# An MLP up projection in seven products: the next pair's first product put ahead of the last two, and its side work spread out

## The chip, the cores and the metric

One core of a Trainium2 chip runs the whole kernel. The metric is the device time of one execution in microseconds (us); lower is better. The kernel is compared before and after one edit, each as the median of several runs.

## The reference

One layer of a decoder with two branches (a gated linear recurrence and sparse attention), their merge, an output projection, and then an MLP, over 1024 prompt rows and 32 sample rows in float32. The edit touches the MLP alone:

```
x = x + m @ w_o
h2 = _rmsnorm(x, norm2)
x = x + jnp.square(jax.nn.relu(h2 @ w_up)) @ w_down
```

h2 is 1056 x 1024, w_up 1024 x 4096, w_down 4096 x 1024. A last RMSNorm follows.

## The kernel before

Everything is held transposed: features on the 128 partitions, the T = 1056 tokens along the free dimension. float32 products are made of three float32r products: each operand is split into a high part (a cast, on ScalarE) and a low part (the value less the high part, on VectorE), and high x high, high x low and low x high are added in PSUM.

The up projection uses a scheme with 7 products for 2 x 2 blocks in place of 8. The four blocks are the two halves of the contraction (512 features each) by the two halves of the tokens (TH = 528). The operands on the token side (OPS) are made once by `combine`: for each of 4 steps of the contraction 7 combinations of the blocks, split into high and low, 28 tiles in all; those of step 0 and the P1 of step 1 lie in h2a, those of step 3 in h2b, the rest in tiles of their own, which the trace calls h2P. So a run of P1 reads h2a in 6 of its 12 matmuls, that of any other product in 3.

The loop runs over 16 pairs of 128 output features. For pair i two raw blocks of w_up are loaded (`up_raw`, on SP's queue), four sums or differences of their quarters are taken on VectorE (`up_sums`, tiles ws), and seven weight tiles are split (`up_split`). Weight tile g may be split once product g - 6 is done, since there are six buffers. A pair's seven products stand in ORDER: P1, P2, P6, P5, P7, P4, P3. Each is made for two chunks of TC = 264 tokens, 4 steps x 3 matmuls a chunk: a run of 12 matmuls, 168 matmuls a pair.

PSUM has three kinds of tiles here. pua holds two banks, one for each chunk; P1 goes there, and P6, P7 and P4 add to it, one behind the other. pub (one tile a chunk) takes P2; puc (one a chunk) takes P5 and then P3 on top. There are two tiles of each kind, so two pua, with two banks each. After P1, P6 and P7 ScalarE copies the running sum out (tile uu, line 1307), and VectorE builds the output from it: hd0 low = P2 + the copy of P1 (line 1309), hd1 high = P5 + the copy of P7 (1311), hd1 low from the sum in pua after P4, through relu and times rb2 (1313), hd0 high = P3 + the copy of P6 (1315). rb2 is the RMSNorm factor of the token, from `rb_chunk` (tile rb2p, which in the stage's start takes one of the pua places). Then hd is multiplied by rb2 with relu where that is still due (1339), squared (1340) and stored (1341), and the down projection reads it back.

The programmer's listing is not the order of an engine's queue. The framework's planner takes, by its own cost model, the first instruction in the listing that is ready; instructions in `high_priority` go ahead. It also puts in the waits, and it counts a tile of PSUM as one: the first matmul into either bank of pua waits for the last copy in the listing ahead of it, out of either bank. SBUF tiles called U are places of one size, given back to the end of a list and taken from its front.

Of the kernel before, what the change touches and what calls it, by code (L numbers as in the profile page):

```python
# [10 lines left out]
F32 = mybir.dt.float32  # L11
F32R = mybir.dt.float32r
# [30 lines left out]
ORDER = ("P1", "P2", "P6", "P5", "P7", "P4", "P3")  # L43

# [44 lines left out]
def hybrid_step(ctx: ExitStack, tc, x_prompt, x_sample, cache_k, cache_v, cache_idx_k, state_hgrn,  # L89
# [20 lines left out]
    def ps_s(name):  # L110
        return psum.tile([128, 2, 512], F32, name=name, tag="s", bufs=2)
# [1048 lines left out]
    def up_raw(i):  # L1160

        rs_ = []
        for h in range(2):
            if h == 1 and i % 2 == 0:
                r = wp.tile([128, 4, 256], F32, name="wu1", tag="wr", bufs=1)
            else:
                r = U.get([128, 4, 256], F32, "wu0")
            nc.sync.dma_start(r, w_up[0][h * 512:(h + 1) * 512, i * 256:(i + 1) * 256]
                              .rearrange("(k p) m -> p k m", p=128))
            rs_.append(r)  # L1170
        return rs_
# [3 lines left out]
    for j in (0, 4, 1, 5, 2, 6, 3, 7):  # L1175
# [3 lines left out]
        if j == 7:  # L1179
            raw[0] = up_raw(0)  # L1180
# [36 lines left out]
    def up_sums(i):  # L1217

        r = raw[i]
        s12, s34 = (U.get([128, 2, 4, 128], F32, "ws") for _ in range(2))  # L1220
        a11, a21 = r[0][:, :, :128], r[0][:, :, 128:]
        a12, a22 = r[1][:, :, :128], r[1][:, :, 128:]
# [5 lines left out]
        return ({"P1": a11, "P2": a12, "P6": s12[:, 1], "P5": s12[:, 0], "P7": s34[:, 0], "P4": a22, "P3": s34[:, 1]},  # L1228
                [s12, s34, r[0]] + ([r[1]] if i % 2 else []))

    SRC = {}
    wus = Ring(U, 2)
    us = Ring(U, 2)
    W = {}

    def up_split(g):

        i, q = g // 7, ORDER[g % 7]
        if g % 6 < 4:
            w = wp.tile([128, 2, 4, 128], F32R, name="wu" + q, tag=("wl", "wh")[g % 6 // 2], bufs=2)  # L1240
        else:
            w = wus.get([128, 2, 4, 128], F32R, "wu" + q)
        with tc.high_priority():
            nc.scalar.copy(w[:, 0], SRC[i][0][q])
            nc.vector.tensor_tensor(w[:, 1], SRC[i][0][q], w[:, 0].bitcast(F32), op=ALU.subtract)
        W[g] = w
        if g % 7 == 6:
            U.put(*SRC[i][1])
# [12 lines left out]
    SRC[0] = up_sums(0)  # L1261
    for g in range(6):
        up_split(g)
    raw[1] = up_raw(1)
# [7 lines left out]
    for i in range(16):  # L1272
        pa = ps_s("pua")
        pb, pc = [ps_g("pub") for _ in range(2)], [ps_t("puc") for _ in range(2)]
        banks = [{"P1": pa[:, c, :TC], "P2": pb[c][:, :TC], "P5": pc[c][:, :TC]} for c in range(2)]
        for c in range(2):
            banks[c]["P6"] = banks[c]["P7"] = banks[c]["P4"] = banks[c]["P1"]
            banks[c]["P3"] = banks[c]["P5"]
        uu = [us.get([128, 4, TC], F32, "uu") for _ in range(2)]
        hd = [U.get([128, T], F32, f"hd{e}") for e in range(2)]  # L1280

        def product(q, c, ks):
            ps = banks[c][q]
            sl = slice(c * TC, (c + 1) * TC)
            for k in ks:
                x, w = OPS[k, q], W[i * 7 + ORDER.index(q)]
                for n_, (a, b) in enumerate(((0, 0), (0, 1), (1, 0))):
                    nc.tensor.matmul(ps, w[:, a, k], x[:, b, sl], start=(q in "P1P2P5" and k == n_ == 0),  # L1288
                                     stop=(k == 3 and n_ == 2), skip_group_check=True)

        if i == 0:

            for q in ("P1", "P2", "P5"):
                for c in range(2):
                    product(q, c, range(3))
            prb = ps_s("rb2p")
            for c in range(2):
                rb_chunk(prb[:, c, :CH], slice(c * CH, (c + 1) * CH))
        for n, q in enumerate(ORDER):
            for c in range(2):  # L1300
                ps = banks[c][q]
                sl = slice(c * TC, (c + 1) * TC)
                s2 = slice(TH + c * TC, TH + (c + 1) * TC)
                product(q, c, (3,) if i == 0 and q in ("P1", "P2", "P5") else range(4))
                with tc.high_priority():
                    if q in ("P1", "P6", "P7"):
                        nc.scalar.copy(uu[c][:, "P1P6P7".index(q) // 2], ps)  # L1307
                    if q == "P2":
                        nc.vector.tensor_tensor(hd[0][:, sl], ps, uu[c][:, 0], op=ALU.add)
                    elif q == "P7":  # L1310
                        nc.vector.tensor_tensor(hd[1][:, s2], banks[c]["P5"], uu[c][:, 2], op=ALU.add)
                    elif q == "P4":
                        nc.vector.scalar_tensor_tensor(hd[1][:, sl], ps, 0.0, rb2[:, sl], op0=ALU.max, op1=ALU.mult)
                    elif q == "P3":
                        nc.vector.tensor_tensor(hd[0][:, s2], ps, uu[c][:, 1], op=ALU.add)
            if i == 0 and n == 2:
                rb_chunk(prb[:, 0, :CH], slice(2 * CH, T))
            if i * 7 + n + 6 < 112:
                up_split(i * 7 + n + 6)
            if n == 0 and i < 15:  # L1320
                if i < 14:
                    raw[i + 2] = up_raw(i + 2)
                SRC[i + 1] = up_sums(i + 1)
            if i == 15:
                for k in range(4):
                    if 8 <= k * 7 + n < 21:
                        U.put(OPS[k, q])
                if n == 0:
                    lo0 = hid_load(0, lambda e, a: U.get([128, T], F32R, "hdl"))
                elif n == 1:  # L1330
                    hi0 = [U.get([128, T], F32R, "hdh") for _ in range(4)]
                    for l_, h_ in zip(lo0, hi0):
                        hid_split(l_, h_)
                elif n < 6:
                    x1_again(2)
                if n == 5:
                    wd0 = wload(w_down[0, :512, :], 0, 4, 256, "wd")
# [115 lines left out]
```

## Time and profile before

| | |
|---|---|
| median of 3 runs | 1837.68 us (1835.46 to 1846.53) |
| the profiled execution | 1841.7 us, span of the trace 1840.0 us |
| mean granted TensorE clock | 0.982 |
| TensorE busy | 1755.7 us (95%) |
| VectorE, ScalarE busy | 1145.2 us (62%), 767.3 us (42%) |
| up projection, first to last matmul | about 1091.9 to 1447.1 us |

A busy engine in the profile has an instruction in it; TensorE's instructions overlap, so that a matmul is shown for 0.28 us where one starts each 0.12 us. Idle time stands with the instruction that came behind it, and with it what released that instruction. A line such as L1288 is a line of the kernel.

### The profile page before, as it was taken

The numbers are of one execution on the slowest core, as the hardware profiler recorded it, in microseconds if no ns is written. First come the engines' busy times: TensorE is split into PE (matmuls) and PEld (weight loads), VectorE is DVE, ScalarE is ACT, GpSimd is POOL, SyncE is SP. The second block draws the span as 40 slices with busy tenths as digits, with TensorE's granted clock in tenths as the row PEclk, the third lists the DMA queues.
The fourth block names the chain that finished last, engine by engine and source line by source line (L and its number), as shares of the span: only waits on it lengthen the run. The fifth ranks groups of instructions, "written<-read, shape, count | busy, mean of one in ns | idle before, by whom it ended". The sixth has DMA issues, their size and how long they took to land.

```text
span 1840.0 us, 29018 instructions
## 1 busy us (share of the span) xinstructions
PE 1755.7 (95%) x11644; PEld 1693.3 (92%) x11644; DVE 1145.2 (62%) x2534; ACT 767.3 (42%) x1330; POOL 188.1 (10%) x212
## 2 busy tenths in 40 slices
PE   6999999998999989979999999999999999999997
PEld 5999999998999988867899999999999899999997
DVE  7276485645799897955646668555555634444435
ACT  5456465244578822343523554333333501111112
POOL 1100000022000015631100330000000000000000
PEclk8999999899999999989999999999999999999999
DMA  4411121231223224542543332332223712222212
GB/s 152 139 50 47 48 63 53 54 86 34 80 76 100 71 82 134 178 161 71 157 137 104 105 128 71 108 114 94 94 94 100 300 58 94 94 94 94 93 46 95
DMA packets 135846, 181.78 MB, mean 99 GB/s; under 512 B 9056, under 2 KB 111232, under 8 KB 135712
## 3 DMA queue, kind: packets, MB, share of 16 engines
q1 hardware_dynamic: 115232, 125.88, 21.3%
q0 software_dynamic: 13424, 44.87, 7.9%
q10 hardware_dynamic: 7056, 9.18, 1.4%
q8 instruction: 91, 1.49, 0.3%
q14 instruction: 43, 0.35, 0.1%
HBM read 128.96 MB, written 48.11 MB: 96 GB/s over the span
## 4 chain that ended last, share of the span: by engine, by line
PE 46%; DMA 6%; DVE 4%; issue 4%; ACT 2%; POOL 2%; SPq 0%; DVEq 0%; ACTq 0%; POOLq 0%
PE pua L1288 10%; PE pd L144 6%; PE pd L146 6%; PE pd L145 6%; PE puc L1288 5%; PE pub L1288 2%; PE po L146 2%; PE po L145 2%; PE po L144 2%; DMA qb<-q_d 2%; DMA hdn<-hid_d 1%; POOL qb L889 1%; PE po L856 1%; DMA vpg<-in_cache_v_dram,ids 1%; PE wap L144 1%
## 5 line engine op out<-in xcount | busy, mean ns | idle before, releaser
L144 PE MATMUL pd<-hdn,wdh 128*128 128x352 f32 (+3 forms) x672 | 218.9, 326 | 3.0 <-DVE x L1381 2.8
L145 PE MATMUL pd<-hdn,wdh 128*128 128x352 f32 (+3 forms) x672 | 215.7, 321 | 0.0
L146 PE MATMUL pd<-hdn,wdl 128*128 128x352 f32 (+3 forms) x672 | 215.6, 321 | 0.0
L1381 DVE TENSOR_TENSOR x<-x,pd 128x352 f32<-128x352 f32 (+3 forms) x192 | 99.7, 519 | 174.6 <-PE pd L146 174.5
L144 PEld LDWEIGHTS pd<-hdn,wdh 128*128 128x128 f32 x672 | 126.2, 188 | 6.0 <-DVE x L1381 4.7
L145 PEld LDWEIGHTS pd<-hdn,wdh 128*128 128x128 f32 x672 | 126.3, 188 | 1.2
L146 PEld LDWEIGHTS pd<-hdn,wdl 128*128 128x128 f32 x672 | 126.0, 188 | 1.3
L144 PE MATMUL wgt<-hh,wgth 128*128 128x352 f32 x384 | 126.6, 330 | 0.0
L146 PE MATMUL wgt<-hh,wgtl 128*128 128x352 f32 x384 | 124.8, 325 | 0.0
L145 PE MATMUL wgt<-hl,wgth 128*128 128x352 f32 x384 | 124.6, 325 | 0.0
L136 ACT CAST wdh<-wdr 128x1024 fp32r<-128x1024 f32 x28 | 29.5, 1053 | 215.9 <-PE pd L145 206.3
L1288 PE MATMUL pua<-h2P,wuP 128*128 128x264 f32 x672 | 102.9, 285 | 0.0
L1288 PE MATMUL pua<-h2a,wuP 128*128 128x264 f32 x480 | 83.2, 292 | 14.0 <-ACT uu L1307 12.7
L747 ACT ACTIVATE jkA<-sc,bstg 128x1024 bf16<-128x1024 bf16 (+5 forms) x93 | 87.3, 939 | 19.6 <-DVE bstg L766 6.8
L1288 PEld LDWEIGHTS pua<-h2P,wuP 128*128 128x128 f32 x672 | 90.6, 189 | 0.0
L1288 PEld LDWEIGHTS pua<-h2a,wuP 128*128 128x128 f32 x480 | 67.2, 189 | 20.5 <-ACT uu L1307 19.1
L742 DVE TENSOR_SCALAR_CACHE_REDUCE jkD<-sc,bstg 128x768 bf16<-128x768 f32 (+3 forms) x96 | 84.4, 879 | 1.1
L1307 ACT COPY uu<-pua 128x264 f32<-128x264 f32 x96 | 36.3, 378 | 109.5 <-PE pua L1288 85.1
L144 PEld LDWEIGHTS wgt<-hh,wgth 128*128 128x128 f32 x384 | 72.1, 188 | 2.5 <-issue 1.7
L145 PEld LDWEIGHTS wgt<-hl,wgth 128*128 128x128 f32 x384 | 72.3, 188 | 1.4 <-issue 0.5
L146 PEld LDWEIGHTS wgt<-hh,wgtl 128*128 128x128 f32 x384 | 72.2, 188 | 1.4 <-issue 0.8
L1288 PE MATMUL pua<-h2b,wuP 128*128 128x264 f32 x384 | 68.7, 286 | 1.8 <-DVE h2b L1139 1.8
(782 smaller groups left out, 4954.1 us busy)
## 6 DMA issues: line engine op xcount, KB each, us to landing
hid_d<-hd SPq DMA_DIRECT2D x32, 528.0 KB, 2.7
wu<-in_w_up_dram SPq DMA_DIRECT2D x32, 512.0 KB, 3.9
wdr<-in_w_down_dram SPq DMA_DIRECT2D x32, 512.0 KB, 3.4
hdn<-hid_d SPq DMA_DIRECT2D x28, 528.0 KB, 4.6
sg_d<-gst ACTq DMA_DIRECT2D x48, 176.0 KB, 2.4
wgtr<-in_w_in_dram SPq DMA_DIRECT2D x16, 512.0 KB, 3.9
qb<-q_d POOLq DMA_DIRECT2D x16, 512.0 KB
wasg<-sg_d SPq DMA_DIRECT2D x8, 528.0 KB, 5.0
```

The costliest lines, as they stand in the source:

```text
L136: nc.scalar.copy(wh, raw)
L144: nc.tensor.matmul(ps, wh, xh, start=(k == 0), stop=False)
L145: nc.tensor.matmul(ps, wh, xl, start=False, stop=False)
L146: nc.tensor.matmul(ps, wl, xh, start=False, stop=(k == n - 1))
L742: nc.vector.tensor_scalar(jkD[:, 0, :L], SC[i], s if isinstance(s, float) else s[:, a:a + 1], 0.0, op0=op, op1=ALU.add, accum_out=out[:, a ...
L747: nc.scalar.activation(jkA[:, 0, :(i + 1) * 128], src(i), AF.Sign, bias=thr[:, a:a + 1], accum_out=cnt[:, a:a + 1])
L856: nc.tensor.matmul(po[:, :128], vt[:, j, :], pT[:, j, :], start=(j == 0), stop=(j == i))
L889: nc.gpsimd.tensor_tensor(qb, kp[:, 1:2, :].to_broadcast([128, 2, 512]), qb, op=ALU.mult)
L1288: nc.tensor.matmul(ps, w[:, a, k], x[:, b, sl], start=(q in "P1P2P5" and k == n_ == 0), stop=(k == 3 and n_ == 2), skip_group_check=True)
L1307: nc.scalar.copy(uu[c][:, "P1P6P7".index(q) // 2], ps)
L1381: nc.vector.tensor_tensor(x1[:, sl], x1[:, sl], ps, op=ALU.add)
```

## The change

The seven products of all pairs become one list, SEVEN: P1 of pair 0, then for each pair P2, P6, P5, P7, P1 of the next pair, P4, P3. Weight tiles follow this list. uu becomes two tiles that stay for the whole stage, one a chunk, with four places: P6 and P7 have one each, and P1 has two, used in turn. The tiles of the sums (s12, s34) stay as well, and the four sums of the next pair are taken one at a time behind P2, P6, P5 and P7. The two raw loads of a pair are asked for separately: the first behind the next P1, the second behind P3. The products with rb2 and the squares are made for each half of hd as soon as it is there, behind P2, P7, P4 and P3, and a store follows P4 (hd1) and P3 (hd0).

```diff
+SEVEN = [(0, "P1")] + [(i + (q == "P1"), q) for i in range(16) for q in ("P2", "P6", "P5", "P7", "P1", "P4", "P3")
+                       if not (i == 15 and q == "P1")]
...
-    us = Ring(U, 2)
+    uu = [U.get([128, 4, TC], F32, "uu") for _ in range(2)]
+    s12, s34 = (U.get([128, 2, 4, 128], F32, "ws") for _ in range(2))
...
+    def up_sum(i, n):
+
+        p = parts(i)
+        o, x, y, op = (("P5", "a21", "P4", ALU.add), ("P6", "P5", "P1", ALU.subtract),
+                       ("P7", "P1", "a21", ALU.subtract), ("P3", "P2", "P6", ALU.subtract))[n]
         with tc.high_priority():
-            nc.vector.tensor_tensor(s12[:, 0], a21, a22, op=ALU.add)
-            nc.vector.tensor_tensor(s12[:, 1], s12[:, 0], a11, op=ALU.subtract)
-            nc.vector.tensor_tensor(s34[:, 0], a11, a21, op=ALU.subtract)
-            nc.vector.tensor_tensor(s34[:, 1], a12, s12[:, 1], op=ALU.subtract)
+            nc.vector.tensor_tensor(p[o], p[x], p[y], op=op)
...
-        i, q = g // 7, ORDER[g % 7]
+        i, q = SEVEN[g]
...
-    raw[1] = up_raw(1)
+    up_raw(1, 0)
+    up_raw(1, 1)
...
+    def bank(i, q, c):
+
+        if q in ("P1", "P6", "P7", "P4"):
+            if (i, 0) not in BANK:
+                t = ps_s("pua")
+                BANK[i, 0] = [t[:, e, :TC] for e in range(2)]
+            return BANK[i, 0][c]
...
+    def relu2(i, e, sl, scaled):
+        t = hd[i][e][:, sl]
+        if not scaled:
+            nc.vector.scalar_tensor_tensor(t, t, 0.0, rb2[:, sl], op0=ALU.max, op1=ALU.mult)
+        nc.scalar.activation(t, t, AF.Square)
...
+    for g, (i, q) in enumerate(SEVEN):
+        if q == "P2":
+            hd[i] = [U.get([128, T], F32, f"hd{e}") for e in range(2)]
+        for c in range(2):
...
+            product(g, c, (3,) if g in (0, 1, 3) else range(4))
+            ps, u1 = bank(i, q, c), 3 * (i % 2)
+            with tc.high_priority():
+                if q in ("P1", "P6", "P7"):
+                    nc.scalar.copy(uu[c][:, {"P1": u1, "P6": 1, "P7": 2}[q]], ps)
...
+        if g + 6 < len(SEVEN):
+            up_split(g + 6)
+        if 1 <= g % 7 <= 4 and g // 7 < 15:
+            up_sum(g // 7 + 1, g % 7 - 1)
+
+        p = g // 7 + (g % 7 == 5)
+        for h in {0: (0, 1) if g == 0 else (1,), 5: (0,)}.get(g % 7, ()):
+            if p < 16 and (h == 0 or p % 2):
+                U.put(raw[p][h])
+            if p + 2 < 16:
+                up_raw(p + 2, h)
+        if q in ("P2", "P7", "P4", "P3"):
+            e, sl = {"P2": (0, LO), "P7": (1, HI), "P4": (1, LO), "P3": (0, HI)}[q]
+            relu2(i, e, sl, q == "P4")
+            if q in ("P4", "P3"):
+                nc.sync.dma_start(hid_d[2 * i + e], hd[i][e])
+                U.put(hd[i][e])
...
-        for e, sl in ((1, slice(TH, T)), (0, slice(0, T))):
-            nc.vector.scalar_tensor_tensor(hd[e][:, sl], hd[e][:, sl], 0.0, rb2[:, sl], op0=ALU.max, op1=ALU.mult)
-            nc.scalar.activation(hd[e], hd[e], AF.Square)
-            nc.sync.dma_start(hid_d[2 * i + e], hd[e])
-            U.put(hd[e])
```

What the last pair did besides, loading the first part of the down projection, stands behind the same products of the list, counted from its end.

## Rows read from the trace of the kernel before

**Rows 1.** The page, its first part: busy time and share of each engine.

```profile
PE 1755.7 (95%) x11644; PEld 1693.3 (92%) x11644; DVE 1145.2 (62%) x2534; ACT 767.3 (42%) x1330; POOL 188.1 (10%) x212
```

**Rows 2.** Windows: start, 13 pairs, end. Columns: stretch, length, busy time by engine.

```profile
1091.90:1134.96 43.06, 39.73 (x297) 37.81 (x295) 40.78 (x76) 22.45 (x48) 3.10 (x1) 0.96 0.29 100
...
1134.96:1416.85 281.89, 272.04 (x2187) 267.58 (x2186) 160.60 (x274) 107.11 (x195) 0.00 (x0) 1.00 0.30 99
...
1416.85:1447.15 30.30, 27.70 (x218) 26.64 (x217) 16.36 (x26) 12.35 (x19) 4.01 (x8) 1.00 0.63 234
```

**Rows 3.** Groups by line, 1134.96 to 1416.85: busy us, mean ns, idle before.

```profile
L1288 PE MATMUL pua<-h2a,wuP 128*128 128x264 f32 x390 | 67.0, 290 | 9.9 <-ACT uu L1307 9.9
...
L1244 ACT CAST wuP<-ws 128x512 fp32r<-128x512 f32 x52 | 32.3, 622 | 38.9 <-PE pub L1288 17.8 <-DVE ws L1225 13.7 <-PE puc L1288 6.9
...
L1340 ACT ACTIVATE hd<-hd 128x1056 f32<-128x1056 f32 x26 | 28.3, 1087 | 19.5 <-DVE hd L1339 19.5
...
L1224 DVE TENSOR_TENSOR ws<-wu,wu 128x512 f32<-128x512 f32 x13 | 8.9, 688 | 0.2
```

**Rows 4.** Waits, same stretch: waiter, releaser, us in total, times, longest.

```profile
ACT uu L1307 <- DVE hd L1315: 22.7, 13, 2.0
...
PE pua L1288 <- ACT uu L1307: 9.9, 21, 0.5
```

**Rows 5.** Timeline of TensorE, about one pair: start, us, engine, line, idle before.

```profile
1214.82 0.88 PE L1288 MATMUL pua<-h2a,wuP 128*128 128x264 f32 x6
...
1216.26 0.53 PE L1288 MATMUL pua<-h2a,wuP 128*128 128x264 f32 x3
...
1218.35 0.63 PE L1288 MATMUL pua<-h2a,wuP 128*128 128x264 f32 x3 [0.47 <-ACT uu L1307]
...
1220.55 0.63 PE L1288 MATMUL pua<-h2a,wuP 128*128 128x264 f32 x3 [0.47 <-ACT uu L1307]
...
1222.12 0.78 PE L1288 MATMUL pub<-h2a,wuP 128*128 128x264 f32 x5
...
1225.05 0.52 PE L1288 MATMUL pua<-h2a,wuP 128*128 128x264 f32 x3
...
1226.51 0.53 PE L1288 MATMUL puc<-h2a,wuP 128*128 128x264 f32 x3
...
1227.97 0.52 PE L1288 MATMUL pua<-h2a,wuP 128*128 128x264 f32 x3
```

**Rows 6.** Timeline of ScalarE, same stretch.

```profile
1217.92 0.38 ACT L1307 COPY uu<-pua 128x264 f32<-128x264 f32 x1 [0.55 <-PE pua L1288]
1220.12 0.38 ACT L1307 COPY uu<-pua 128x264 f32<-128x264 f32 x1 [1.82 <-PE pua L1288]
...
1229.33 0.38 ACT L1307 COPY uu<-pua 128x264 f32<-128x264 f32 x1 [1.72 <-DVE hd L1315]
```

**Rows 7.** Timeline of TensorE, the stage's end (the first form three times).

```profile
1433.86 0.63 PE L1288 MATMUL pua<-h2a,wuP 128*128 128x264 f32 x3 [0.47 <-ACT uu L1307]
...
1445.58 0.64 PE L1288 MATMUL pua<-h2a,wuP 128*128 128x264 f32 x3 [1.19 <-DVE hd L1313]
```

**Rows 8.** Timeline of TensorE, the stage's start.

```profile
1104.20 0.52 PE L1288 MATMUL pua<-h2b,wuP 128*128 128x264 f32 x2 [1.75 <-DVE h2b L1139]
...
1108.79 0.96 PE L1288 MATMUL pua<-h2a,wuP 128*128 128x264 f32 x3 [0.47 <-ACT uu L1307]
...
1118.10 0.75 PE L1126 MATMUL rb2p<-sqs,ones 128*128 128x352 f32 x2
...
1128.26 0.63 PE L1288 MATMUL pua<-h2a,wuP 128*128 128x264 f32 x3 [0.51 <-ACT uu L1307]
```

**Rows 9.** The page, its sixth part: DMA issues, KB each, us to landing.

```profile
hid_d<-hd SPq DMA_DIRECT2D x32, 528.0 KB, 2.7
wu<-in_w_up_dram SPq DMA_DIRECT2D x32, 512.0 KB, 3.9
```

**Rows 10.** Forms of line 1339: ns at least, median, most; shapes.

```profile
L1339 DVE SCALAR_TENSOR_TENSOR hd<-hd,sqs x32: 702/980/1259, 1129.4 to 1446.9; 128x528 f32<-128x528 f32 x16, 128x1056 f32<-128x1056 f32 x16
```

More of the change, by code (lines that the diff above doesn't have):

```diff
@@ L1158, in combine, with up_raw @@
             split(dst["P3"], h1[:, hi], sl)
[L1160 to L1171, printed above, removed]
+    def up_raw(i, h):
+        if h == 1 and i % 2 == 0:
+            r = wp.tile([128, 4, 256], F32, name="wu1", tag="wr", bufs=1)
+        else:
+            r = U.get([128, 4, 256], F32, f"wu{h}")
+        nc.sync.dma_start(r, w_up[0][h * 512:(h + 1) * 512, i * 256:(i + 1) * 256].rearrange("(k p) m -> p k m", p=128))
+        raw.setdefault(i, []).append(r)
     X1 = {}
@@ L1179, in hybrid_step @@
         if j == 7:
-            raw[0] = up_raw(0)
+            up_raw(0, 0)
+            up_raw(0, 1)
         for c in range(NCH):
@@ L1259, in hid_split @@
         nc.vector.tensor_tensor(lo, lo.bitcast(F32), hi.bitcast(F32), op=ALU.subtract)
-    SRC[0] = up_sums(0)
+    for n in range(4):
+        up_sum(0, n)
+    up_raw(1, 0)
+    up_raw(1, 1)
     for g in range(6):
         up_split(g)
-    raw[1] = up_raw(1)
     X2 = []
@@ L1270, in x1_again @@
             nc.gpsimd.dma_start(X2[-1], x1_d[len(X2) - 1])
[L1272 to L1275, printed above, removed]
-        for c in range(2):
[L1277 to L1283, printed above, removed]
-            sl = slice(c * TC, (c + 1) * TC)
[L1285 to L1337, printed above, removed]
-        for e, sl in ((1, slice(TH, T)), (0, slice(0, T))):
-            nc.vector.scalar_tensor_tensor(hd[e][:, sl], hd[e][:, sl], 0.0, rb2[:, sl], op0=ALU.max, op1=ALU.mult)
-            nc.scalar.activation(hd[e], hd[e], AF.Square)
-            nc.sync.dma_start(hid_d[2 * i + e], hd[e])
-            U.put(hd[e])
@@ new lines, in hybrid_step, with product @@
+    prb = ps_s("rb2p")
+    BANK, hd = {}, {}
+    def bank(i, q, c):
[4 more added lines that the diff above has]
+            return BANK[i, 0][c]
+        k = 1 if q == "P2" else 2
+        if (i, k) not in BANK:
+            BANK[i, k] = [(ps_g("pub") if k == 1 else ps_t("puc"))[:, :TC] for _ in range(2)]
+        return BANK[i, k][c]
+    def product(g, c, ks):
+        i, q = SEVEN[g]
+        ps = bank(i, q, c)
+        sl = slice(c * TC, (c + 1) * TC)
+        for k in ks:
+            x, w = OPS[k, q], W[g]
+            for n_, (a, b) in enumerate(((0, 0), (0, 1), (1, 0))):
+                nc.tensor.matmul(ps, w[:, a, k], x[:, b, sl], start=(q in "P1P2P5" and k == n_ == 0),
+                                 stop=(k == 3 and n_ == 2), skip_group_check=True)
@@ new lines, in relu2 @@
+    def relu2(i, e, sl, scaled):
[3 more added lines that the diff above has]
+        nc.scalar.activation(t, t, AF.Square)
+    for g in (0, 1, 3):
+        for c in range(2):
+            product(g, c, range(3))
+    for c in range(2):
+        rb_chunk(prb[:, c, :CH], slice(c * CH, (c + 1) * CH))
+    LO, HI = slice(0, TH), slice(TH, T)
+    for g, (i, q) in enumerate(SEVEN):
+        if q == "P2":
+            hd[i] = [U.get([128, T], F32, f"hd{e}") for e in range(2)]
+        for c in range(2):
+            sl = slice(c * TC, (c + 1) * TC)
+            s2 = slice(TH + c * TC, TH + (c + 1) * TC)
+            product(g, c, (3,) if g in (0, 1, 3) else range(4))
[3 more added lines that the diff above has]
+                    nc.scalar.copy(uu[c][:, {"P1": u1, "P6": 1, "P7": 2}[q]], ps)
+                if q == "P2":
+                    nc.vector.tensor_tensor(hd[i][0][:, sl], ps, uu[c][:, u1], op=ALU.add)
+                elif q == "P7":
+                    nc.vector.tensor_tensor(hd[i][1][:, s2], bank(i, "P5", c), uu[c][:, 2], op=ALU.add)
+                elif q == "P4":
+                    nc.vector.scalar_tensor_tensor(hd[i][1][:, sl], ps, 0.0, rb2[:, sl], op0=ALU.max, op1=ALU.mult)
+                elif q == "P3":
+                    nc.vector.tensor_tensor(hd[i][0][:, s2], ps, uu[c][:, 1], op=ALU.add)
+        if g == 2:
+            rb_chunk(prb[:, 0, :CH], slice(2 * CH, T))
+        if g + 6 < len(SEVEN):
[14 more added lines that the diff above has]
+                U.put(hd[i][e])
+        if g >= 103 and i == 15:
+            for k in range(4):
+                if 8 <= k * 7 + ORDER.index(q) < 21:
+                    U.put(OPS[k, q])
+        if g == 105:
+            U.put(s12, s34)
+            lo0 = hid_load(0, lambda e, a: U.get([128, T], F32R, "hdl"))
+        elif g == 106:
+            hi0 = [U.get([128, T], F32R, "hdh") for _ in range(4)]
+            for l_, h_ in zip(lo0, hi0):
+                hid_split(l_, h_)
+        elif 107 <= g <= 110:
+            x1_again(2)
+            if g == 110:
+                wd0 = wload(w_down[0, :512, :], 0, 4, 256, "wd")
@@ L1345, in hybrid_step @@
     wus.close()
-    us.close()
+    U.put(*uu)
     nf = U.get([128, 1024], F32, "nf")
```

18 lines of the change are left out of this document (7 added, 11 removed).

## The prediction

> **What bounds the kernel now.** I read the page's busy shares first: TensorE has 1755.7 of 1840.0 us, VectorE 62%, ScalarE 42% [rows 1]. So the whole is TensorE's, and a change here is worth only what TensorE idles in the stage that it touches, the up projection. Next the windows of that stage [rows 2]: its start (43 us, clock 0.96), its 13 undisturbed pairs (281.89 us, or 21.68 us a pair, clock 1.00) and its end (30.3 us). In the 13 pairs VectorE works 160.60 / 13 = 12.4 us a pair and ScalarE 107.11 / 13 = 8.2 us, so neither is near its limit, and DMA is 30% busy.
>
> Then the groups of the 13 pairs [rows 3]. TensorE's idle time before its products stands in one group alone: 9.9 us before the matmuls of pua on h2a, released by the copy of line 1307. The waits count them: 21 times, 0.5 us at most [rows 4]. What one costs is more than its idle time, as the timeline shows [rows 5]: a run of 12 matmuls (one product, one chunk) takes 1226.51 - 1225.05 = 1.46 us; a run that begins and ends at such a wait takes 1220.55 - 1218.35 = 2.20 us. So a stall costs 0.74 us (0.63 up to the late start, and 0.11 because the first two matmuls behind it start further apart). 13 pairs of 168 matmuls at 1.46 / 12 = 0.1217 us are 265.8 us; 21 stalls at 0.74 are 15.5; together 281.3 of the 281.89 measured. There is nothing else to win there.
>
> Why they stall is seen in the same rows. A stall comes where a run in pua follows another run in pua with nothing between: the copy starts when the run has ended (1217.92), takes 0.38 us, and the next run starts at 1218.35; then the same again at 1220.12 and 1220.55 [rows 5, 6]. Where a run in pub or puc lies between (from 1222.12, from 1226.51) the next run in pua shows no wait. Both chunks of a pair share one pua tile, and the program waits for the last copy out of the tile, whichever chunk it read. So a pair is a chain of eight runs in pua: P1, P6, P7, P4, two chunks each, and six other runs (P2, P5, P3) to lay between.
>
> One more row matters: a run that reads h2a in 6 of its 12 matmuls is a P1 (two of its four operands lie there). The one at 1214.82 is the next pair's P1, which the planner had already pulled ahead [rows 5]. It was of little use: its copy came at 1229.33, after a wait for the sum of P3, line 1315 [rows 6], as 13 of these copies did, 22.7 us in all [rows 4]. The copy goes to a uu tile that is taken anew for each pair, so it can't start before the pair ahead has read its own.
>
> **The change, part by part.**
>
> The order, and uu with a place of its own for every second P1: the next P1 may be copied out while the pair ahead still holds its uu, and it stands in the listing between P7 and P4, the place where two products in a row had only pua to go on with. Now each product in pua has one beside it in another tile: P6 has P5, P7 has P1 of the other pua tile, P4 has P3, and P2 lies between pairs. A run between is 1.46 us; what it must cover is 0.74 us, or 0.74 + 0.62 = 1.36 us when ScalarE has just begun a cast [rows 3]. Stalls outside the first and the last pair: the 21 above and 2 of the same form ahead of that stretch (the first at 1128.26 [rows 8]), 23 x 0.74 = 17.0 us. Bounds: all gone, 17.0, or half of them, 8.9. I take 21 gone, 15.5 us, near the upper end, since no run with another between shows a stall in rows 5.
>
> The end: the last pair has no P1 to put ahead. Before, three stalls of the usual form and one of 1.19 us idle behind the VectorE read of P4's first chunk [rows 7], 3 x 0.74 + 1.45 = 3.7 us (1.45: 1.19 idle, 0.16 because a matmul is shown for 0.28 us and takes 0.12 of the pace, 0.10 as above). Now P5 and P3 can still lie between, but P7 to P4 can't be covered. Bounds 0 and 3.7; I keep two stalls and gain 2.2 us.
>
> The start: P1 of pair 1 takes its pua tile at the sixth product, not the eighth, and the tile is the one that the rb2p matmuls use until 1118.10 [rows 8]. Until then P7 and P4 of pair 0 have no cover: up to three stalls, -2.2 us, while the stalls of before there (1.75 and 0.47 us idle) come from h2b and stay; at best the one of 0.47 goes, +0.7. I take -1.2, nearer to the loss, because the start is where VectorE is full (40.78 of 43.06 us busy [rows 2]) and nothing comes early.
>
> The sums: as many as before, four of 0.69 us a pair on VectorE [rows 3], one behind each product instead of four in a burst. In place, in two tiles that stay, so a sum waits for the split that read the last pair's value one or more products ago. Nothing in TensorE's time; the cover is the six weight buffers, which hold five products (14.6 us) ahead of the one that runs. The raw loads: 32 as before, on SP, 3.9 us to landing [rows 9], each asked for some eight products (23 us) ahead of its first use; behind them in SP's queue stand the hid_d stores only. Cost 0; if the cover is gone the price is the landing, 3.9 us once.
>
> The squares and products with rb2: ScalarE squares of 1056 take 1.087 us and casts of 512 take 0.622 [rows 3], which gives 0.855 ns an element and 0.64 us for 528, so four of them are 2.54 against 2 x 1.087 = 2.17: +0.37 us a pair. VectorE: 0.702 for 528 and 1.259 for 1056 [rows 10], so 3 x 0.70 = 2.11 against 1.96: +0.15 us. Both lie beside TensorE (8.6 and 12.5 us of some 20.6 a pair). What they can do is stand in front of a copy: 0.64 us, which the 1.46 us cover; half covered it is 0 to -3 us over the stage, and I take 0, since a cast of 0.62 us stands there already.
>
> Sum: 15.5 + 2.2 - 1.2 = 16.5 us. The profiled execution took 1841.7 us (1840.0 of span and 1.7 around it), 4.0 above the median; it would take 1825.2. Against the median of 1837.7 the forecast is **1821 us**. The ends of the terms give 17.0 + 3.7 + 0.7 = 21.4 us (1816) and 8.9 + 0 - 2.2 - 3 = 3.7 us (1834).
>
> **The rivals.**
>
> *Nothing is gained (1835 to 1840).* The planner had already pulled the next P1 ahead, so the new order may only write down what it did. Against it: the copy's wait for line 1315 [rows 4], which the places in uu take away. A second way to the same end is that tiles of PSUM are short: then the stalls stay whatever the order, as the change adds no tile and needs both pua tiles at once for longer. By the rows the stalls end with a copy out of the tile in use, 21 of 21 [rows 4], and none with the release of an older one. The Trainium skill (Perfetto Trace Analysis, Optimization Strategy) says that the same gap repeating on the engine that should be saturated can mean too little SBUF or PSUM for the next tile; by that rule the gain here would be 0, and the trace doesn't agree. Chance 0.08 for both.
>
> *Slower: chunk behind chunk.* The shared pua tile makes each second chunk wait for the copy of the first. If TensorE's queue follows the listing, a pair has four such places with nothing between (P6, P7, P1, P4): 64 x 0.74 = 47.4 us against the 27 x 0.74 = 20.0 of now, +27 us, 1865. It gets slower from 1.7 stalls a pair on, and by over 1% from 52 in all, 3.2 a pair. Against it: in rows 5 the queue does not follow the listing, P2 and P3 lie between chunks. For it: more of the order is now fixed by what each product needs. Chance 0.10, 1845 to 1865.
>
> *A store in the way (1829 to 1838).* The next pair's first hd tile takes a place that was given back after P4, whose store must have landed. From the end of P4 to the end of the next P2's first chunk lie P3 and that chunk, 3 x 1.46 = 4.4 us. The store is out after 0.43 for the product, 0.64 for the square and 2.7 us to landing [rows 9], 3.8 us, plus whatever SP has before it. If it is late, VectorE stands at the sum behind P2 (line 1309) with the splits queued behind. VectorE has 8 us a pair to spare, so it takes over 8 us, or a copy held by it, to reach TensorE; one stall a pair, 16 x 0.74 = 11.8 us, leaves a gain of 4.7, 1833. Chance 0.10.
>
> **How the numbers follow.** The forecast 0.70 (1816 to 1834, most of it below 1828), nothing gained 0.08, slower 0.10, the store 0.10, below 1816 0.02. A range of 1815 to 1838 leaves out the slower case, half of nothing gained and the little below: 0.16. What a measurement of this kernel can tell from no change is about 1%, 18.4 us, so 1819.3: the forecast lies 2 us above it, and some 0.29 of its 0.70 below it, with the 0.02 faster 0.31. Slower by over 1% (1856) is most of the slower case, 0.09 with a little for what I didn't think of. Within 1%: 0.60.
>
> **What would show it.** Right: in the 13 middle pairs at most one or two waits of pua for the uu copy, 20.5 to 20.7 us a pair, no copy of P1 that waits for the sum of P3, P1's copy within some 1 us of its run. Start and end: two or three stalls each. Wrong: the same number of 0.47 us waits (nothing gained), over two a pair at second chunks (slower), or VectorE waiting for a store with ScalarE's casts idle behind it. A change in the down projection's start, whose loads run at 234 GB/s in the last window [rows 2], would be a term that I left at 0.

## The result and the profile after

The changed kernel takes 1817.32 us, the median of 6 runs (1815.7 to 1824.21), against 1836.08 for the kernel before on the same chip (6 runs, 1832.9 to 1846.53): 18.8 us less, a ratio of 0.9893 with a 95% interval of 0.9872 to 0.9913. The forecast was 1821. The profiled execution after has a span of 1814.1 us, 25.9 less than that of before. TensorE's line of the page, which answers to [rows 1]:

```profile
PE 1745.5 (96%) x11644; PEld 1689.5 (93%) x11644; DVE 1143.2 (63%) x2550; ACT 772.0 (43%) x1362; POOL 186.3 (10%) x212
```

The windows of the stage, cut as in [rows 2] into start, 13 pairs and end:

```profile
1083.75:1126.88 43.13, 41.65 (x316) 39.24 (x315) 41.13 (x76) 24.89 (x55) 0.95 (x1) 1.00 0.31 99
1126.88:1394.00 267.12, 267.12 (x2193) 267.12 (x2192) 158.46 (x289) 111.34 (x222) 0.00 (x0) 1.00 0.32 111
1394.00:1418.12 24.12, 23.65 (x192) 23.29 (x191) 15.64 (x26) 12.35 (x21) 4.01 (x8) 1.00 0.63 225
```

The middle is what to look at: TensorE is busy for all of its 267.12 us, and 2193 matmuls in them are 0.1218 us each, the pace of a run without a wait. A pair takes 20.5 us where it took 21.68. The waits of the whole stage, 1083.75 to 1418.12 (waiter, releaser, us in total, times, longest), answer to [rows 4]:

```profile
ACT uu L1323 <- PE pua L1297: 80.7, 78, 2.6
...
DVE hd L1325 <- DMA hid_d<-hd: 5.3, 6, 1.5
...
PEld pua L1297 <- ACT uu L1323: 2.8, 5, 0.8
...
PE pua L1297 <- ACT uu L1323: 1.7, 4, 0.6
```

The copies of uu (now line 1323) wait for TensorE alone. No row has them waiting for the sum of P3, where 13 of them waited 22.7 us [rows 4]. TensorE waits for a copy four times. The timeline of TensorE shows where, and a stretch of the middle:

```profile
1096.08 0.64 PE L1297 MATMUL pua<-h2a,wuP 128*128 128x264 f32 x3 [0.22 <-ACT uu L1323]
...
1098.63 0.63 PE L1297 MATMUL pua<-h2a,wuP 128*128 128x264 f32 x3 [0.56 <-ACT uu L1323]
...
1120.05 0.63 PE L1297 MATMUL pua<-h2a,wuP 128*128 128x264 f32 x3 [0.47 <-ACT uu L1323]
...
1219.65 0.53 PE L1297 MATMUL pua<-h2a,wuP 128*128 128x264 f32 x3
1220.02 0.89 PE L1297 MATMUL pua<-h2P,wuP 128*128 128x264 f32 x6
1220.74 0.53 PE L1297 MATMUL pua<-h2b,wuP 128*128 128x264 f32 x3
1221.10 0.53 PE L1297 MATMUL pua<-h2a,wuP 128*128 128x264 f32 x3
...
1410.70 0.63 PE L1297 MATMUL pua<-h2a,wuP 128*128 128x264 f32 x3 [0.47 <-ACT uu L1323]
```

A run in pua still follows a run in pua at 1221.10, and there is no wait: such neighbours now lie in the two pua tiles of two pairs. In the order of TensorE's queue, as the built programs have it, 28 runs stood directly behind a run in the same pua tile before, and 4 do after. Three of the four waits left are in the first two pairs and one in the last.

The pieces of the side work cost what was forecast (groups by line and form, 1126.88 to 1394.00; mean ns behind the bar):

```profile
L1304 ACT ACTIVATE hd<-hd 128x528 f32<-128x528 f32 x53 | 34.1, 644 | 23.1 <-DVE hd L1303 23.1
...
L1303 DVE SCALAR_TENSOR_TENSOR hd<-hd,sqs 128x528 f32<-128x528 f32 x40 | 27.9, 700 | 0.1
```

**Where the time went.** In the table below the stage runs from its first product matmul to the first matmul of pd. "Over pace" is the time of a part less 0.1217 us for each of its matmuls: the first two pairs (336 matmuls), the 13 in the middle (2184) and the last (168). The last part ends with the first matmul of pd, so it holds what TensorE waits for that one; this wait stands by itself under "pd". "Waits" are TensorE's for a copy of uu. "Down" runs from the first matmul of pd to its last. "At 0.50" is how long TensorE's granted clock was at 0.50, the lower of its two levels (1.2 GHz), in a part; in the middle it never was, and at all other times from the stage's start to the last matmul of pd it was 1.00 (2.4 GHz). All are worked out from the start times of the matmuls and the records of the clock in each trace; the kernels of the experiments stand in the same table.

```
                     stage   over pace, us          pd   waits      down    at 0.50, us
                     us      first2  mid13   last   us   us    n    us      first2 last down
before               355.24   7.98   16.10   4.03   0    12.7  27   382.04   3.4   0    0
control_before       355.58   7.88   16.09   4.48   0    12.7  27   383.07   3.4   0    0
after                334.28   5.64    0.54   0.97   0     1.7   4   385.18   0     0    3.4
after_again          334.67   5.65    0.92   0.97   0     1.7   4   384.21   0     0    0
spread_only          355.94   7.01   15.66   6.15   0    15.6  29   384.08   0     3.4  0
order_uu             334.05   5.66    0.48   0.78   0     1.7   4   389.07   0     0    6.8
uu_only              342.06   7.72    1.08   6.14   3.6   3.1   4   388.98   3.4   1.3  8.9
uu_stays_one_place   342.09   7.56    1.08   6.32   3.4   3.0   4   387.88   3.4   0.7  9.6
p1_own_tile          341.31   7.68    0.47   6.03   3.9   2.6   3   383.98   3.4   0.7  6.1
p1_last              337.44   5.66    0.44   4.21   3.3   2.0   5   389.74   0     0   10.2
both_chunks_before   344.16   5.77    1.04  10.22   0     5.2   3   388.15   0     6.8  6.8
both_chunks_after    335.43   6.81    0.44   1.05   0     2.1   2   385.44   3.4   0    3.4
late_copy            337.56   6.40    2.33   1.70   0     3.6   7   382.99   0     0    0
in_listing           388.04  13.56   44.35   3.00   0    27.3  49   385.10   3.4   0    3.4
```

The stage is 355.24 - 334.28 = 20.96 us shorter: 15.56 in the middle, 3.06 in the last pair, 2.34 in the first two. The down projection gives 3.14 back. That makes 17.8, near the 18.8 of the medians. The other 8 us of the two profiled spans lie ahead of the stage, where both programs have the same instructions. There the clock was at 0.50 for 54.6 us before and for 37.6 after; half of the difference is 8.5 us.

The clock is in two of the terms as well. At 0.50 the matmuls of before start 0.88 / 4 = 0.22 us apart:

```profile
1106.80 1.08 PE L1288 MATMUL pub<-h2a,wuP 128*128 128x264 f32 x4
1107.68 0.64 PE L1288 MATMUL pua<-h2b,wuP 128*128 128x264 f32 x2
```

Before has 3.41 us of it in its first two pairs, soon behind the wait of 1.75 us for h2b [rows 8]; 0.47 us of them are a wait, so they cost some (3.41 - 0.47) / 2 = 1.5 us, which is in the 2.34. After has none there, but 3.41 us in its down projection, behind a wait of 1.95 us for an add to x: some 1.7 us, which is in the 3.14. The second look at after has none in either place.

### The profile page after: what moved, and what is told of

The parts are those of the page before. It is cut to its first block, busy times and chain, and to the rows that moved or that the text cites. A ratio compares the mean times of both kernels' runs of the same rounds, so it can differ in the third digit from the quotient of the medians.

```text
span 1814.1 us, 29069 instructions
## 1 busy us (share of the span) xinstructions
PE 1745.5 (96%) x11644; PEld 1689.5 (93%) x11644; DVE 1143.2 (63%) x2550; ACT 772.0 (43%) x1362; POOL 186.3 (10%) x212
## 4 chain that ended last, share of the span: by engine, by line
PE 82%; DMA 6%; DVE 5%; issue 3%; POOL 2%; ACT 2%; SPq 0%; DVEq 0%; ACTq 0%; POOLq 0%
PE pua L1297 10%; PE pd L147 6%; PE pd L149 6%; PE pd L148 6%; PE puc L1297 5%; PE pub L1297 2%; PE lev L506 2%; PE wgt L147 2%; PE wgt L149 2%; PE wgt L148 2%; DMA qb<-q_d 2%; PE po L149 2%; DMA hdn<-hid_d 2%; PE po L148 2%; PE po L147 2%
## 5 line engine op out<-in xcount | busy, mean ns | idle before, releaser
L1297 PE MATMUL pua<-h2a,wuP 128*128 128x264 f32 x480 | 79.1, 286 | 1.7 <-ACT uu L1323 1.7
L1248 DVE TENSOR_TENSOR wuP<-ws,wuP 128x512 fp32r<-128x512 f32 x64 | 43.8, 687 | 39.8 <-ACT wuP L1247 39.4
```

What stands on the lines that cost most here:

```text
L1248: nc.vector.tensor_tensor(w[:, 1], src, w[:, 0].bitcast(F32), op=ALU.subtract)
```

## The experiments

The theory of the forecast was that the new order and the freed uu together clear the stalls, and that the spreading is free. Its rivals: the order alone does it; the copy's hold alone is the cause; the second place for P1 is needed; the two chunks that share a pua tile are the cause. Three groups were run, each beside the kernel before on its own chip (medians 1845.95 of 31 runs, 1847.35 of 24 and 1838.57 of 11), so ratios are compared, and stages from the table.

**Does the stage repeat?** Both kernels unchanged, once more.

> The kernel before, unchanged, profiled again for a second look at what of its time is its own. Every theory: 27 waits of pua for the uu copy and about 355 us from the first product to the first matmul of the down projection. Open is the rest: if the 8 us by which the changed kernel came to the up projection earlier, and the 382 us of the down projection, are a matter of the execution, they come out otherwise here by some us.

> The changed kernel, unchanged, beside the three below and with more rounds. Every theory: 4 waits of pua for the uu copy, 334.3 us to the down projection. Open: the down projection, 382.0 and 383.1 us in the two looks at the kernel before and 385.2 in the one at the changed kernel. If what it gave back belongs to the change, some 385 us again; if to the execution, between 382 and 390.

The kernel before: 1842.42 us in one run, its stage 0.34 us from the first look. The kernel after: 1822.15, a ratio of 0.9905 (0.9883 to 0.9927), its stage 0.39 us from the first look. A stage is therefore known to some half a microsecond, far better than a whole run. The two rows that matter in the waits of control_before's stage are those of before:

```profile
ACT uu L1307 <- DVE hd L1315: 24.4, 14, 2.0
...
PE pua L1288 <- ACT uu L1307: 12.7, 27, 0.5
```

**The parts alone.** First the spreading of sums, loads and squares, with the old order and the old uu:

```
# for each pair, in the loop over its seven products
-            if n == 0 and i < 15:
-                if i < 14:
-                    raw[i + 2] = up_raw(i + 2)
-                SRC[i + 1] = up_sums(i + 1)
+            if n < 4 and i < 15:
+                up_sum(i + 1, n)
...
+            if q in ("P2", "P7", "P4", "P3"):
+                e, sl = {"P2": (0, LO), "P7": (1, HI), "P4": (1, LO), "P3": (0, HI)}[q]
```

> The kernel before with the sums, the raw loads, the products with rb2 and the squares spread as in the change (the tiles of the sums stay), but the order of the products and the uu taken anew for each pair as before. Cover theory and uu theory: nothing, 24 to 30 waits of pua, 1834 to 1838 us. Spreading theory: the gain, under 10 waits, 1816 to 1822 us.

1849.24 us, a ratio of 1.0019 (0.9988 to 1.0049), and a stage of 355.94. The spreading is worth nothing by itself. Its waits tell more than that:

```profile
ACT uu L1308 <- DVE hd L1316: 4.2, 12, 0.4
...
PE pua L1289 <- ACT uu L1308: 15.6, 29, 2.8
```

ScalarE's wait for the sum of P3 has shrunk from 24.4 us to 4.2, and TensorE waits as often as before. So the length of that wait was not what TensorE paid for. The copy itself is held as long: from pair 2 on the copy of P1's first chunk starts 9.5 to 13.2 us behind the start of its run's last matmul, where before it was 10.5 to 13.5. A square now stands on ScalarE in front of it (at 1225.45 us, the copy at 1226.45), and what is left of the wait is short.

Then the other way about, the new order and uu without the spreading:

```
-        if 1 <= g % 7 <= 4 and g // 7 < 15:
-            up_sum(g // 7 + 1, g % 7 - 1)
+        if g % 7 == 1 and g // 7 < 15:
+            for n in range(4):
+                up_sum(g // 7 + 1, n)
...
-        if q in ("P2", "P7", "P4", "P3"):
+        if q == "P3":
+            for e, sl in ((1, HI), (0, slice(0, T))):
```

> The changed kernel with the list of products and the uu that stays, but the sums in one burst behind P2, both raw loads behind P3, and the products with rb2 and the squares at the end of the pair as before. Cover theory: the whole gain, 4 to 6 waits of pua, 1816 to 1820 us. uu theory: the same. Spreading theory: the gain is lost, 20 to 27 waits, 1832 to 1838 us.

1831.78, 0.9923 (0.9894 to 0.9953), with a stage of 334.05, the same as after. The gain of the stage comes whole without the spreading.

Next uu alone, with a place of its own for every second P1, in the old order:

```
-    us = Ring(U, 2)
+    uu = [U.get([128, 4, TC], F32, "uu") for _ in range(2)]
...
-                        nc.scalar.copy(uu[c][:, "P1P6P7".index(q) // 2], ps)
+                        nc.scalar.copy(uu[c][:, {"P1": 3 * (i % 2), "P6": 1, "P7": 2}[q]], ps)
```

> The kernel before, with nothing changed but uu: two tiles that stay, P1 with two places used in turn. Cover theory: the copies of P1 no longer wait for line 1315, but P7 to P4 stays without cover; 14 to 20 waits of pua, 3 to 8 us gained, 1828 to 1833 us. uu theory: most of the gain, 4 to 8 waits, 1817 to 1821 us. Spreading theory: no gain, 27 waits, 1835 to 1838 us.

1835.63, 0.9935 (0.9908 to 0.9961). The middle is cured (16.10 to 1.08 us over pace) without the new order. The ends stay dear, 7.72 and 6.14, but not for the copies alone: the first holds a stretch at clock 0.50, as before, and of the last 3.6 us are a wait behind all the products, for ScalarE's cast of the down projection's first operand:

```profile
PE pd L144 <- ACT hdh L1258: 3.6, 1, 3.6
```

And the new uu with the next P1 listed last of its group, so that it stands behind P3:

```
-SEVEN = [...  for q in ("P2", "P6", "P5", "P7", "P1", "P4", "P3") ...
+SEVEN = [...  for q in ("P2", "P6", "P5", "P7", "P4", "P3", "P1") ...
```

> The changed kernel with the next pair's P1 listed behind P3 again (P2, P6, P5, P7, P4, P3, P1); uu that stays, the spread sums, loads and squares are kept. Cover theory (the listing puts a run in another tile beside each run in pua; order and the uu that stays are both needed): the 0.47 us waits of pua for the uu copy come back, about one a pair at P7 to P4, 14 to 20 in all, and 10 to 15 us of the 18.8 us are lost: 1828 to 1834 us. uu theory (the planner pulls P1 ahead by itself once its copy is not held): 4 to 6 waits, 1816 to 1819 us. Spreading theory (bursts on VectorE and ScalarE were what made the copies late): also 1816 to 1819 us.

1832.27, 0.9917 (0.989 to 0.9944), with 5 waits for a copy where the forecast's own theory expected 14 to 20. The middle is 0.44. The last pair is 4.21 where after has 0.97, but it has the same single wait of 0.47 us for a copy; the rest is a wait behind all the products, for the cast of the down projection's first weights:

```profile
PE pd L147 <- ACT wdh L139: 3.3, 1, 3.3
```

Without it the stage is 334.15, that of after. So no run shows a gain in the stage from the place between P7 and P4.

**What of uu is it?** Two kernels on the one before. The first keeps the two uu tiles for the whole loop, with one place for P1, in the same memory as before:

```
-    us = Ring(U, 2)
+    uu = [U.get([128, 4, TC], F32, "uu") for _ in range(2)]
...
-        uu = [us.get([128, 4, TC], F32, "uu") for _ in range(2)]
```

> The kernel before with uu as two tiles that stay for the whole stage, and nothing else: P1 has one place, as before, not two in turn. Hold theory (what cost the time was that a uu tile taken anew waits for the last reader of the old one, so P1's copy waited for P3's sum): as with two places, 4 to 6 waits of pua, 341 to 343 us to the down projection, since the one place is read by P2 long before. Two-places theory (P1 needs the second place): the waits come back, 15 to 27, 350 to 355 us.

1836.24, 0.9942 (0.9914 to 0.9971); the stage is 342.09, as with two places. The second place does nothing here. The waits of its stage have no row of a copy for the sum of P3, and this for TensorE:

```profile
PE pua L1287 <- ACT uu L1306: 3.0, 4, 1.7
```

The second takes tiles anew for each pair, but P1's copy has one of its own, whose last reader is the sum of P2:

```
-        uu = [us.get([128, 4, TC], F32, "uu") for _ in range(2)]
+        u1 = u1s.get([128, 2, TC], F32, "uu1")
+        u67 = u67s.get([128, 2, 2, TC], F32, "uu")
```

> The kernel before with the copies in other tiles, both still taken anew for each pair: one for P1 (both chunks), whose last reader is P2's sum, and one for P6 and P7 (both chunks), whose last reader is P3's sum. Hold theory: P1's copy no longer waits for P3's sum, so 4 to 6 waits of pua, 341 to 343 us. If what mattered was that tiles aren't renewed at all (the planner's bookkeeping): 20 to 27 waits, 352 to 355 us.

1834.39, 0.9932 (0.9906 to 0.9957), the middle at 0.47. Taking a tile anew was not the harm. The harm was that the last reader of the whole tile was the sum of P3, so the next P1's copy stood behind it.

**Is the shared pua tile part of it?** Both chunks' matmuls are listed ahead of both copies, in each kernel, so that the second chunk no longer waits for the copy of the first:

```
                 product(q, c, (3,) if i == 0 and q in ("P1", "P2", "P5") else range(4))
+            for c in range(2):
+                ps = banks[c][q]
+                sl = slice(c * TC, (c + 1) * TC)
+                s2 = slice(TH + c * TC, TH + (c + 1) * TC)
                 with tc.high_priority():
```

> The kernel before with the copies and sums of a product listed behind the matmuls of both its chunks, not chunk by chunk, so that a second chunk no longer waits for the copy of the first. Chain theory (the eight runs in pua are one chain because the tile counts as one, and the hold on P1's copy only makes it too long): the waits fall to under 10, 338 to 345 us to the down projection. If the hold alone sets them: still 14 or more waits, now at P1 to P6 and P7 to P4, 345 to 355 us.

> The changed kernel with copies and sums listed behind the matmuls of both chunks, so that no second chunk waits for the copy of the first. Chain theory: the middle has nothing left to give (0.54 us), so 0 to 1 us there; the last pair, where P7 and P4 have no cover, gains at most one wait of two, or loses as in the kernel before with the same edit (10.2 us in its last pair). 333 to 341 us to the down projection, the time within 1% of the changed kernel. If the shared tile still cost something: 330 us or less, and faster.

On the kernel before: 1840.0, 0.9957 (0.9934 to 0.9979). The middle falls from 16.10 to 1.04, with the old uu and the old order; the last pair gets dearer (10.22), with fewer and longer waits, and with 6.8 us at clock 0.50 behind them:

```profile
PE pua L1288 <- ACT uu L1311: 5.2, 3, 2.7
...
PE puc L1288 <- DVE hd L1319: 1.6, 1, 1.6
```

On the kernel after: 1818.92, 0.9906 (0.9879 to 0.9934), beside 0.9905 for after itself. Nothing is left for it to win.

**Does the new order need the new uu?** The kernel after, with P1's copy moved behind the sum of P3, into the place of P6, so that it must wait for that sum again:

```
-            ps, u1 = bank(i, q, c), 3 * (i % 2)
+            ps, u1 = bank(i, q, c), (i + 1) % 2
...
-                if q in ("P1", "P6", "P7"):
-                    nc.scalar.copy(uu[c][:, {"P1": u1, "P6": 1, "P7": 2}[q]], ps)
+                if q in ("P6", "P7") or g == 0:
+                    nc.scalar.copy(uu[c][:, {"P1": 1, "P6": i % 2, "P7": 2}[q]], ps)
...
-                    nc.vector.tensor_tensor(hd[i][0][:, s2], ps, uu[c][:, 1], op=ALU.add)
+                    nc.vector.tensor_tensor(hd[i][0][:, s2], ps, uu[c][:, i % 2], op=ALU.add)
+                    if i < 15:
+                        nc.scalar.copy(uu[c][:, i % 2], bank(i + 1, "P1", c))
```

> The changed kernel with the hold put back: P1 of the next pair is copied out behind the sum of P3, into the place of P6's copy that this sum reads, so that it must wait for it as before. P1, P6 and P7 stay two chunks each in one pua tile; the two chunks of P1 alone no longer wait for each other. Cover theory as forecast (the order gives every run in pua a run beside it): the order is enough by itself, at most 4 waits of pua and 1 us over the pace in the 13 middle pairs, since P2 lies between the copy and P6; 334 to 336 us. Hold theory in its strict form (the copy's wait for P3's sum is what costs, whatever the order): 15 waits or more, 345 to 355 us.

1820.08, 0.991 (0.9884 to 0.9936). The waits of its stage show TensorE hardly touched, and two timelines show the copy held: the run of a P1's first chunk starts at 1203.58, its copy (line 1333) at 1216.59:

```profile
PE pua L1297 <- ACT uu L1323: 3.6, 7, 0.9
ACT uu L1333 <- DVE hd L1331: 2.6, 9, 0.3
...
1203.58 0.89 PE L1297 MATMUL pua<-h2a,wuP 128*128 128x264 f32 x6
...
1216.59 0.38 ACT L1333 COPY uu<-pua 128x264 f32<-128x264 f32 x1 [0.30 <-DVE hd L1331]
```

The middle is 2.33 over pace, not 16: some 1.8 us more than after. One thing more differs here: P1's copies now stand behind both its chunks, so its second chunk has no copy to wait for. How much the new order would do without that is not shown. The theory that the held copy alone makes the stalls falls here, as the one that only the new order clears them fell with uu_only.

**The price of a queue that follows the listing.** The kernel after, with each run (one product, one chunk) tied behind the run listed before it, from pair 1 on:

```
+        with (tc.issue_after(LAST[0]) if LAST and g > 7 else ExitStack()):
             for k in ks:
...
+        LAST[:] = [mm.ins]
```

> The changed kernel with TensorE's queue tied to the listing from pair 1 on: each run may be put only behind the run listed before it, so that the planner can no longer lay other runs between the two chunks of P6, P7, P1 and P4. No operation differs. The rival of the prediction (chunk behind chunk): 4 waits a pair, 15 x 4 = 60 of them at 0.74 us, 44 us more than the changed kernel: 376 to 380 us to the down projection and 1855 to 1863 us by the changed kernel's 1817. If the chip covers such a wait otherwise (a wait of 0.47 us is partly made up behind it): under 360 us.

1870.47 (1868.44 to 1872.99), 1.0171 (1.0149 to 1.0194): slower than the kernel before. The waits of TensorE in its stage, and two of them in its timeline:

```profile
PE pua L1298 <- ACT uu L1325: 27.3, 49, 0.9
...
PE pua L1298 <- DVE hd L1331: 8.9, 15, 0.6
```

```profile
1203.33 0.53 PE L1298 MATMUL pua<-h2b,wuP 128*128 128x264 f32 x3
1204.33 0.63 PE L1298 MATMUL pua<-h2a,wuP 128*128 128x264 f32 x3 [0.47 <-ACT uu L1325]
...
1210.63 0.52 PE L1298 MATMUL pua<-h2b,wuP 128*128 128x264 f32 x3
1211.76 0.63 PE L1298 MATMUL pua<-h2a,wuP 128*128 128x264 f32 x3 [0.60 <-DVE hd L1331]
```

49 waits for a copy and 15 for VectorE's read of P4's first chunk: 64, the number of the rival's sum. Those for the copy begin the next run 1204.33 - 1203.33 = 1.00 us after three matmuls began, 0.63 above the usual 0.37; those for VectorE 1.13, 0.76 above. With the slower start of the run behind (0.11) that is 0.74 and 0.87.

## Why the prediction was right

**The middle, 15.5 us forecast, 15.56 measured.** This is the term that carried the forecast, and its size was right: 21 stalls at 0.74 us, all gone. The credit was too narrow. The forecast gave it to the order and uu together. The runs show that the middle's stalls needed three things at once: the next P1's copy behind the last reader of a whole uu tile, two chunks that the program counts as one pua tile, and the old listing. Where one of them was taken away, 2.33 us or less of the 16.10 were left:

- the copy set free: uu_only 1.08, uu_stays_one_place 1.08, p1_own_tile 0.47;
- the chunks listed together: both_chunks_before 1.04;
- the listing changed and the copy still held: late_copy 2.33 (there P1's second chunk is free as well, so the listing alone is not shown).

That the planner finds another run to lay between once the copy is free is read from its queues: 4 runs stand directly behind another in the same tile in uu_only, p1_own_tile and p1_last, against 28 before and in spread_only. In both_chunks_before it lays none between: 67 stand so, but 65 of them are second chunks, which have no copy ahead of them to wait for. In late_copy it is 21, 16 of them second chunks of P1. Why it finds no other run with all three in place is in its choices run by run, and these were not followed.

**The end, 2.2 forecast, 3.06 measured.** Two stalls were to be left, and one is (1410.70). That the order pays here is not shown: p1_last has the same one stall, and uu_only one wait too, of 1.78 us; what makes their last pairs dear is for the most part the wait for pd.

**The start, -1.2 forecast, 2.34 measured.** The sign is wrong, and the stalls are not why: 1.5 of the 2.34 us are the clock. The forecast read a clock of 0.96 in this window [rows 2] and put it at nothing; after shows 1.00. Of the other 0.8, two stalls at 0.74 were booked under the middle's 23 and kept as its margin, which leaves -0.7 for the start itself. Up to three new stalls were allowed for, at P7 and P4 of pair 0, as the pua tile of pair 1 is the one that the rb2p matmuls use. Three are there, but at P6 and P7 of pair 0 (1096.08, 1098.63) and at P6 of pair 1 (1120.05). And the wait of 1.75 us for h2b, which was to stay [rows 8], is not among the waits of TensorE in after. The step that failed is "the stalls of before there come from h2b and stay", and with it the clock. The table bears the clock out: before, control_before, uu_only, uu_stays_one_place and p1_own_tile have the stretch at 0.50 and 7.56 to 7.98 in the first two pairs; after, after_again, order_uu, p1_last and both_chunks_before have none and 5.64 to 5.77. both_chunks_before has the wait of 1.75 us for h2b too, and its clock did not fall; why is open.

**The side work, 0 forecast, 0 measured.** The durations were 644 ns for a forecast 0.64 us and 700 for 0.70. spread_only's stage is 0.36 us above control_before's, and order_uu's 0.23 below after's.

**The down projection, a term left at 0, which gave back 1.1 to 3.1 us** (385.18 and 384.21 against 382.04 and 383.07). Of the 3.14 between the first looks some 1.7 are the stretch at clock 0.50, which after_again does not have, so they belong to the execution. The rest is waits: over the whole down projection TensorE waits 4.6 and 5.0 us in the two looks at before, 6.6 and 5.7 in those at after. The waits just behind the stage of after, and of before, are:

```profile
ACT hdn L1259 <- DMA hdn<-hid_d: 7.1, 8, 1.9
...
PE pd L147 <- DVE x L1405: 2.7, 2, 2.4
DVE hdn L1260 <- ACT hdn L1259: 2.6, 2, 1.8
```

```profile
ACT hdn L1258 <- DMA hdn<-hid_d: 7.4, 6, 2.4
...
DVE hdn L1259 <- ACT hdn L1258: 1.6, 2, 1.2
...
PE pd L144 <- DVE x L1381: 0.5, 1, 0.5
```

TensorE waits for the add to x. On VectorE the add stands behind a split of hdn, which waits for ScalarE's cast, which waits for a load. This chain is read from the trace; no run undid it. It does not go with the stage's gain: late_copy's stage is 17.7 us shorter than before and its down projection takes 382.99, while order_uu has the stage of after and loses 7.0, by another wait:

```profile
ACT wdh L139 <- PE puc L1297: 4.0, 1, 4.0
PE pd L147 <- ACT wdh L139: 3.4, 1, 3.4
```

The clock adds nearly as much again. The windows of order_uu and of after, 35 us from the down projection's start, show it in the third column from the end (the clock), 0.90 and 1.00:

```profile
1419.34:1454.43 35.09, 29.93 (x165) 28.43 (x164) 21.56 (x27) 13.90 (x13) 0.87 (x2) 0.90 0.65 235
...
1418.02:1453.12 35.10, 31.64 (x193) 30.46 (x192) 22.05 (x28) 13.08 (x13) 0.87 (x2) 1.00 0.68 246
```

Over the whole down projection TensorE waits 8.6 us in order_uu, 4.0 more than in before. The wait of 3.4 us is followed by 6.8 us at 0.50, of which 0.7 still lie in it, so the clock costs some 6.1 / 2 = 3.1. Together that is 7.1, for 7.0 measured. What stands on ScalarE around the last pair seems to decide this, but no run changed it alone. It may be why order_uu, with the stage of after, was timed 0.0018 higher in its ratio than after_again; the intervals overlap, and the two were timed on different chips.

**The rivals.** *Nothing gained* fell. The Trainium skill (Perfetto Trace Analysis, Optimization Strategy) says that the same gap repeating on the engine that should be saturated can mean too little SBUF or PSUM for the next tile; here the gap went without a pua tile more, and in uu_stays_one_place with the same two uu tiles, only kept. The trace doesn't agree in this case. *Chunk behind chunk* did not happen, since TensorE's queue does not follow the listing; in_listing shows it as real as it was priced: 64 waits, a time 31.9 us above before, where 27 was forecast. Of the difference, 15 x (0.87 - 0.74) = 2 us are the waits for VectorE; the rest was not followed. *A store in the way* came six times, 5.3 us in all, and stopped at VectorE: no wait of TensorE answers to it.

By the profile the terms are 15.56 + 3.06 + 2.34 - 3.14 = 17.8 us against a forecast of 16.5. The error at the start and the one in the down projection nearly cancel; as the clock is in both, 1.5 us for the change and 1.7 against it, that is luck. Neither late_copy nor both_chunks_after can be told from after by its time, and no run beat it. The small change of uu_only was timed at 0.9935 (0.9908 to 0.9961), after itself at 0.9893 and 0.9905; these intervals overlap too.

## What to carry to other kernels

A tile that is taken anew for each step makes its first writer wait for the last reader of the whole old tile, whichever place that reader wanted; keep the tile and its places, or cut it by last readers, before adding memory. The same holds for a PSUM tile of two banks that the program counts as one: list the matmuls into both banks ahead of both reads. Where several waits make one stall together, lifting one can be enough (here a few lines that keep uu), so try each part of a change alone before crediting all of it, and read the part that moved from its stage, which repeats to 0.4 us where whole runs differ by 10. Before a part is credited with what an end of the stage gained, look there for the clock and for a wait that belongs to what follows.

## What was not expected of the hardware

The same instructions ahead of the stage took different times from one execution to the next: after's stage began at 1083.85 us in one look and at 1093.66 in another, with stages that agree to 0.39 us. The granted clock goes with it: ahead of the stage it was at 0.50 for 37.6 us in the first look and for 54.6 in the second, and half of that difference is 8.5 of the 9.8 us. A single span of this kernel can't judge a change of less than 10 us.

At the down projection's start one wait cost about twice its length. In order_uu, uu_only, uu_stays_one_place, p1_own_tile and p1_last TensorE waits 3.3 to 3.9 us there, and each time the clock is at 0.50 for 6.8 us, from near the end of the wait on: by an estimate some 3 us more. No kernel without such a wait has such a stretch at that place; after's waits of 2.35 and 1.95 us in the down projection had 3.4 us at 0.50 behind the second and none behind the first.

A wait on ScalarE of 24.4 us in the stage could shrink to 4.2 with no gain in TensorE's 12.7 to 15.6, while the copy behind it stayed as late: how long an engine waits for a release said nothing of what the release was worth.
